# Softmax weights times v: from a high/low float32r pair to plain float32, with one PSUM bank per head and a new order of work

## The chip, the cores and the metric

One core of one Trainium2 chip runs the whole layer in one launch. The metric is device time in microseconds (us), the median of repeated executions of the same program. All arithmetic is float32 or close to it: the kernel keeps the precision of float32 products on TensorE by splitting operands into a high and a low part.

## The reference

One layer of a hybrid encoder over 512 positions of 1,024 channels. The parts in full detail below are those that the change touches.

```python
def reference(x, mem, ...):
    h = rms_norm(x, norm_mix_pre)
    z = h @ w_in                                  # 1024 x 6144
    u_s, q, k, v, g = split(z)                    # 1024 each, g 2048
    ys = s5_branch(u_s, ...)                      # 64 groups x 64 complex states, scan over positions
    ys = gelu(ys); ys = ys * sigmoid(ys @ w_glu + b_glu)
    ya = diff_attention(q, k, v, ...)
    merged = g_a * (ys @ w_ssm_proj) + g_b * (ya @ w_da_proj)
    x = x + rms_norm(merged @ w_mix_out, ...)
    x = x + rms_norm(memory_cross_attention(...), ...)      # 4 heads, 256 memory tokens
    x = x + rms_norm(square(relu(rms_norm(x) @ w_ff1)) @ w_ff2, ...)

# diff_attention, 8 heads, two softmaxes of 64 channels each, 128 channels of v, blocks of 128 queries:
    p = softmax(where(k_chunk <= q_chunk, q k^T / 8, -inf))
    w = p[:, :, 0] - lam * p[:, :, 1]
    o = w @ v
    o = o * rsqrt(mean(o * o, axis=-1) + EPS) * head_norm * (1 - lam_init)
```

## The kernel before, in words

Every big product is made of float32r products. An operand X is kept as a high part (X cast to float32r) and a low part (X minus the high part), and a product of two such operands is three products on TensorE (`trip`): high by low, low by high, high by high. Weights stream in from HBM in pieces of 128x1024 (`wload`); ScalarE makes the high part `whi`, VectorE or GpSimd the low part `wlo` (`wsplit`).

The order of work is set while the program is recorded. Each part of the work is a Python generator with a rank; `step` always advances the generator of lowest rank whose next instruction could start, by a table of costs and latencies, no later than a little after the time at which TensorE has come (`SLACK`). The big projections are the filler (`filler`, rank 1000): they go to TensorE whenever nothing of lower rank is ready. The ranks are the constants `R_...`; `BX` and `BW` are biases that decide, phase by phase, whether VectorE or GpSimd takes an operation that both could do; `ULEAD` and `GL` say how many of the u and gate projections stand ahead of and behind each head's q and k projection. Each engine then works through its own list in order, and waits where an operand isn't there. All DMAs are issued by one queue, SyncE's, in order.

The first 400 us or so hold, side by side:

- the projections for v, u, q, k and the gates (48 pieces of weights, 24 products each);
- the S5 branch in eight groups m (`ssm_pre`, `ssm_mid`, `ssm_main`). In `ssm_main` TensorE first multiplies the group's u with a small table (the rows `ps<-u,ga`, 16 float32 products), VectorE scans the states, and TensorE then makes the outputs (`ps<-st,C` and `ps<-u,Dt`, 16 products each). u comes back from HBM in another layout into `u2`, and the table `Dt` comes from HBM too; there is one buffer for each, so a group's loads wait until the group before has made its outputs;
- the differential attention, head by head. `rope` rotates q and k in one pair of buffers (`ropeB`, `ropeA`) and copies the result by DMA into `q02`, `k02` and so on, of which there is one set (`QB = 1`): a head's copies wait until the head before has made its last scores, and k's rotation waits until q's copies have read the buffer. `attn_block` makes the scores of a block of 128 queries, both softmax numerators, their difference `w`, transposes it on TensorE, and multiplies it with v. `attn_head` then sums, normalizes and transposes the head's output.

In weights times v (`attn_block`, from L1031) the transposed weights are split into `wth` (ScalarE) and `wtl` (VectorE), and v was kept as high and low part side by side in the tile `vy` (`evac_v`, `evac_rows`). For each block of 128 keys TensorE makes two products into one PSUM region of 256 columns: `wth` with both parts of v (256 columns), and `wtl` with the high part of v (128 columns). A head has two PSUM banks; `attn_head` copies the second halves out, adds the first halves to them (tile `on`), squares, and brings in the softmax sum `sm0` as a factor: its reciprocal is applied twice to the sum of squares and once to the result. The rsqrt is a power of -1/2 on GpSimd (`rstd`).

After the S5 branch come the gated unit (`glu`; its input is split from `mt` into `g2h` and `g2l` by `gelu`), the merge, the output projection, the cross-attention and the MLP; from about 400 us on the kernel is nearly all large products.

Of the kernel before, what the change touches and what calls it, by code (L numbers as in the profile page):

```python
# [31 lines left out]
HEADS = 8  # L32
# [40 lines left out]
WTB = 2  # L73
# [26 lines left out]
class Kern:  # L100
# [889 lines left out]
    def attn_block(self, pool, h, i, po, sm0, qk, vv, todo, fin):  # L990
        q2, k2 = qk
        km, rows = P * (i + 1), slice(P * i, P * i + P)
        v = self.V
        sm = yield from self.small(4)
        sm1 = yield from self.small(2)
        p = yield from self.alloc(pool, [P, 2, SEQ], "p", bufs=PBUF)
# [26 lines left out]
        w = p[:, 0, :km]  # L1023
# [11 lines left out]
        while len(po) <= i // 2:  # L1035
            po.append((yield from self.bank("o")))
        yield (None, self.rdy(wh, wl, vv))
        o = po[i // 2][:, 2 * P * (i % 2):2 * P * (i % 2) + 2 * P]
# [4 lines left out]
        self.drop(wh, wl)  # L1043
        fin.append(i)

    def attn_head(self, pool, h, Q, yo, vv, ya):
        v = self.V
# [4 lines left out]
        sm0, ss4, rs = sm[:, 0:4], sm[:, 4:8], sm[:, 8:12]  # L1052
        fin, po, todo = [], [], [8]
# [3 lines left out]
        ya[h] = yo  # L1057
        on = yield from self.alloc(pool, [P, 4, P], "on")
# [12 lines left out]
        yield from self.rstd(ss4, 4, 1.0 / P, EPS, rs)  # L1071
        yield from v.tensor_tensor(out=rs, in0=rs, in1=sm0, op=ALU.mult)
        for i in range(4):
            yield from self.A.activation(out=on[:, i], in_=on[:, i], func=AF.Copy, scale=rs[:, i:i + 1])
        self.drop(sm)
# [195 lines left out]
    def build(self):  # L1271
# [8 lines left out]
        vp = self.open("vy")  # L1280
# [396 lines left out]
```

## Time and profile before

| | us |
|---|---|
| median of 3 runs (1103.91 to 1105.7) | 1104.45 |
| the profiled execution's own time | 1103.1 |
| its span, first to last instruction | 1101.2 |
| TensorE busy | 1062.3 (96% of the span) |
| VectorE busy | 696.8 (63%) |
| ScalarE busy | 510.7 (46%) |
| GpSimd busy | 100.7 (9%) |
| mean granted TensorE clock, of full speed | 0.993 |

The profile is one execution, so a sum over its rows is made against 1103.1 us; the median lies 1.35 us above it. A large product of 128x512 takes about 390 ns from start to end, but they overlap: a new one starts every 223 to 227 ns. Engine names in the rows: PE is TensorE (PEld its weight loads), DVE VectorE, ACT ScalarE, POOL GpSimd, SPq the DMA queue of SyncE.

### The profile page before, as it was taken

To read this page: it belongs to the slowest core of one execution; us is meant where nothing else is said; L and a number is where in the kernel's file an instruction comes from. 1 tells how busy PE (TensorE), PEld (TensorE's weight loads), DVE (VectorE), ACT (ScalarE), POOL (GpSimd) and SP (SyncE) were. 2 spreads that over 40 slices of the span, in tenths; PEclk is the share of its full clock that TensorE was granted. 3 is DMA by queue.
4 is the path that set the end of the run, shared out by engine and by line. 5 is a ranking of instruction groups with operands and counts; after the bars stand their busy time and mean duration, and the time that the engine had idled before them with its cause. 6 is when DMAs were issued, how large, how long until landed. Compare 5 with 4: busy or idle time off the path is not lost.

```text
span 1101.2 us, 15716 instructions
## 1 busy us (share of the span) xinstructions
PE 1062.3 (96%) x5854; PEld 884.5 (80%) x5854; DVE 696.8 (63%) x1242; ACT 510.7 (46%) x989; POOL 100.7 (9%) x104
## 2 busy tenths in 40 slices
PE   8999899999979889999999999999999999999997
PEld 7888777787768668888889888889888888888885
DVE  5899999999998777444469555466443223444234
ACT  5556465666556776322256444354432213443121
POOL 5300121012200030000014000011000000000001
PEclk9999999999989999999999999999999999999999
DMA  7556556664545674444555521314333233333222
GB/s 266 163 161 186 153 142 171 168 164 138 158 124 144 169 174 123 144 143 143 191 173 173 173 95 58 99 57 133 98 97 102 99 101 97 96 96 96 96 76 77
DMA packets 96044, 146.38 MB, mean 133 GB/s; under 512 B 45665, under 2 KB 57441, under 8 KB 95969
## 3 DMA queue, kind: packets, MB, share of 16 engines
q1 hardware_dynamic: 95968, 145.39, 44.8%
q8 instruction: 46, 0.75, 0.3%
q14 instruction: 30, 0.24, 0.1%
HBM read 120.87 MB, written 11.91 MB: 121 GB/s over the span
## 4 chain that ended last, share of the span: by engine, by line
PE 71%; DVE 16%; DMA 4%; issue 3%; ACT 3%; SPq 2%; POOL 1%; POOLq 0%; DVEq 0%; ACTq 0%
PE ps L364 70%; DVE rr L95 2%; SPq L215 2%; DVE wlo L95 2%; DVE ga L95 2%; DVE sm L95 2%; DVE ropeA L95 1%; PE ps L373 1%; DMA scr_g<-gt 1%; DMA mt<-scr_y 1%; DVE st L95 1%; DMA Dt<-sk 1%; ACT ropeB L95 1%; DVE ev L95 1%; ACT whi L95 1%
## 5 line engine op out<-in xcount | busy, mean ns | idle before, releaser
L95 DVE TENSOR_TENSOR wlo<-wraw,whi 128x1024 fp32r<-128x1024 f32 x171 | 210.0, 1228 | 278.8 <-ACT whi L95 278.5
L95 ACT CAST whi<-wraw 128x1024 fp32r<-128x1024 f32 (+1 forms) x180 | 185.9, 1033 | 296.0 <-PE ps L364 269.8
L364 PE MATMUL ps<-hTl,whi 128*128 128x512 f32 (+1 forms) x736 | 286.6, 389 | 1.0 <-DVE sm L95 1.0
L364 PE MATMUL ps<-hTh,whi 128*128 128x512 f32 (+1 forms) x736 | 280.9, 382 | 0.0
L364 PE MATMUL ps<-hTh,wlo 128*128 128x512 f32 (+1 forms) x736 | 280.7, 381 | 0.0
L364 PEld LDWEIGHTS ps<-hTh,whi 128*128 128x128 f32 x736 | 138.7, 189 | 27.3
L364 PEld LDWEIGHTS ps<-hTl,whi 128*128 128x128 f32 x736 | 139.0, 189 | 25.8 <-DVE sm L95 1.2
L364 PEld LDWEIGHTS ps<-hTh,wlo 128*128 128x128 f32 x736 | 139.2, 189 | 23.7
L364 PE MATMUL ps<-whi,vy 128*128 128x512 f32 x384 | 123.5, 389 | 0.0
L364 PE MATMUL ps<-whi,g2l 128*128 128x512 f32 x256 | 99.7, 389 | 0.0
L364 PE MATMUL ps<-wlo,vy 128*128 128x512 f32 x224 | 87.9, 392 | 0.0
L364 PEld LDWEIGHTS ps<-whi,vy 128*128 128x128 f32 x384 | 72.1, 188 | 15.1
L364 PE MATMUL ps<-wlo,g2h 128*128 128x512 f32 x192 | 74.9, 390 | 0.0
L364 PE MATMUL ps<-whi,g2h 128*128 128x512 f32 x192 | 74.7, 389 | 0.0
L364 PE MATMUL ps<-vy,whi 128*128 128x512 f32 (+1 forms) x256 | 65.6, 338 | 0.0
L364 PEld LDWEIGHTS ps<-whi,g2l 128*128 128x128 f32 x256 | 48.1, 188 | 9.7
L95 POOL TENSOR_TENSOR sm<-sm,mhalf 128x1 f32<-128x1 f32 (+1 forms) x28 | 25.9, 925 | 326.9 <-DVE sm L95 292.3
L364 PEld LDWEIGHTS ps<-wlo,vy 128*128 128x128 f32 x224 | 42.1, 188 | 8.4
L364 PEld LDWEIGHTS ps<-vy,whi 128*128 128x128 f32 x256 | 44.5, 189 | 5.0
L95 ACT COPY ropeB<-ps 32x512 f32<-32x512 f32 x64 | 37.0, 578 | 14.1 <-DMA q<-ropeB 11.2
L364 PE MATMUL ps<-vy,wlo 128*128 128x512 f32 (+1 forms) x128 | 43.0, 336 | 0.0
L364 PEld LDWEIGHTS ps<-whi,g2h 128*128 128x128 f32 x192 | 36.0, 188 | 7.6
(235 smaller groups left out, 1618.3 us busy)
## 6 DMA issues: line engine op xcount, KB each, us to landing
wraw<-in_wall_dram SPq DMA_DIRECT2D x172, 512.0 KB, 3.5
xr<-in_x_dram SPq DMA_DIRECT2D x8, 512.0 KB, 4.9
q<-ropeB SPq DMA_DIRECT2D x32, 128.0 KB, 3.1
scr_g<-gt SPq DMA_DIRECT2D x16, 256.0 KB, 3.5
Dt<-sk SPq DMA_DIRECT2D x64, 64.0 KB, 3.3
gl<-scr_g SPq DMA_DIRECT2D x16, 256.0 KB, 3.8
gain<-in_gains_dram SPq DMA_DIRECT2D x5, 512.0 KB, 5.3
xt<-in_xT_dram SPq DMA_DIRECT2D x8, 256.0 KB, 5.2
```

The costliest lines, as they stand in the source:

```text
L95: getattr(k.eng[best], "copy" if (best, m) == ("ACT", "tensor_copy") else m)(**kw)
L215: self.nc.sync.dma_start(out=out, in_=in_)
L364: self.nc.tensor.matmul(out, lhsT=lhsT, rhs=rhs, start=start, stop=stop, **kw)
L373: self.nc.tensor.transpose(out, in_, self.ident)
```

## The change

- v is kept once, as float32: `evac_v` scales the PSUM bank by four activations of 128 columns, one per head, and there is no low part. Each head has a tile of its own.
- The transposed weights are copied once by ScalarE into a float32 tile `wt`; `wtl` is gone. For each block of keys TensorE makes one float32 product of 128 columns. A head has one PSUM bank.
- `attn_head` reads that bank directly: no sum of two halves. Squares are taken with a scale of 1/sqrt(128). With s the softmax sum, the result is o * (mean(o^2) + EPS * s^2)^(-1/2), which is the same as dividing o by s first; two small VectorE operations take the place of five.
- The ranks, `SLACK`, `BW` and `ULEAD` have new values, so that the recorded order of the first 400 us differs on every engine.

```diff
-SLACK = 1800.0
+SLACK = 1400.0
-R_TAB, R_PRE, R_ROT, R_MID, R_MAIN, R_U, R_ATT, R_BLK, R_ROPE, R_GATE, R_W = 1, -0.3, -0.55, -0.3, -0.5, 0, 0, 0, 0, 0, -0.55
+R_TAB, R_PRE, R_ROT, R_MID, R_MAIN, R_U, R_ATT, R_BLK, R_ROPE, R_GATE, R_W = 1, 0.1, -0.55, -0.6, -0.5, -0.5, -0.45, 0, 0, -0.3, -0.55
-BW = (1000,400,1000,200,100,400,600,400)
+BW = (200,200,700,200,100,400,600,400)
-ULEAD = (1,2,2,2,1,0,0,0)
+ULEAD = (2,2,2,2,0,0,0,0)
...
-            o = [vv[:, 4 * nh:4 * nh + 4, b, i] for i in range(2)]
-            yield from self.evac_rows(ps.rearrange("p (h e) -> p h e", h=4), o[0], o[1], self.rs[:, b:b + 1])
+            for h in range(4):
+                yield from self.A.activation(out=vv[4 * nh + h][:, b], in_=ps[:, h * P:h * P + P], func=AF.Copy,
+                                             scale=self.rs[:, b:b + 1])
+            self.unbank(ps)
...
-        wh = yield from self.alloc(pool, [P, SEQ], "wth", F32R, bufs=WTB)
-        wl = yield from self.alloc(pool, [P, SEQ], "wtl", F32R, bufs=WTB)
-        yield from self.split(wh[:, :km], wl[:, :km], pt[:, :km])
+        wt = yield from self.alloc(pool, [P, SEQ], "wt", bufs=WTB)
+        yield from self.A.copy(out=wt[:, :km], in_=pt[:, :km])
...
         for kb in range(i + 1):
             c = slice(kb * P, kb * P + P)
-            self.mm(o, wh[:, c], vv[:, kb].rearrange("p x e -> p (x e)"), kb == 0, False)
-            self.mm(o[:, :P], wl[:, c], vv[:, kb, 0], False, kb == i)
+            self.mm(po["b"][:, rows], wt[:, c], vv[:, kb], kb == 0, kb == i)
...
-        for j in range(2):
-            o4 = po[j].rearrange("p (i x e) -> p i x e", i=2, x=2)
-            yield from self.A.copy(out=on[:, 2 * j:2 * j + 2], in_=o4[:, :, 1])
-            yield from v.tensor_tensor(out=on[:, 2 * j:2 * j + 2], in0=o4[:, :, 0], in1=on[:, 2 * j:2 * j + 2], op=ALU.add)
-        self.unbank(*po)
+        o4 = po["b"].rearrange("p (i e) -> p i e", i=4)
...
-            yield from self.A.activation(out=sq, in_=on[:, i], func=AF.Square, accum_out=ss4[:, i:i + 1])
+            yield from self.A.activation(out=sq, in_=o4[:, i], func=AF.Square, scale=P ** -0.5, accum_out=ss4[:, i:i + 1])
...
-        yield from v.reciprocal(out=sm0, in_=sm0)
-        yield from v.tensor_tensor(out=ss4, in0=ss4, in1=sm0, op=ALU.mult)
-        yield from v.tensor_tensor(out=ss4, in0=ss4, in1=sm0, op=ALU.mult)
-        yield from self.rstd(ss4, 4, 1.0 / P, EPS, rs)
-        yield from v.tensor_tensor(out=rs, in0=rs, in1=sm0, op=ALU.mult)
+        yield from v.scalar_tensor_tensor(out=sm0, in0=sm0, scalar=EPS, in1=sm0, op0=ALU.mult, op1=ALU.mult)
+        yield from v.tensor_tensor(out=ss4, in0=ss4, in1=sm0, op=ALU.add)
+        yield from self.G.tensor_tensor(out=rs, in0=ss4, in1=self.mhalf, op=ALU.pow)
```

Three places of the recorded order, before and now.

The start, on VectorE: `hTl` is the low part of a slice of x, `wlo` that of half a piece of weights. Before, GpSimd made the first eight halves of `wlo`, and VectorE began with:

```order
L95 SCALAR_TENSOR_TENSOR hTl_82<-xt_157,vecs_89,hTh_81 128x512
L95 SCALAR_TENSOR_TENSOR hTl_82<-xt_160,vecs_89,hTh_81 128x512
L95 SCALAR_TENSOR_TENSOR hTl_82<-xt_164,vecs_89,hTh_81 128x512
L95 SCALAR_TENSOR_TENSOR hTl_82<-xt_167,vecs_89,hTh_81 128x512
L95 COPY ga_80<-ga_80 128x32
L95 TENSOR_TENSOR ga_80<-ga_80 128x128
```

Now VectorE makes both:

```order
L95 SCALAR_TENSOR_TENSOR hTl_82<-xt_164,vecs_96,hTh_81 128x512
L95 TENSOR_TENSOR wlo_178<-wraw_163,whi_177 128x512
L95 SCALAR_TENSOR_TENSOR hTl_82<-xt_167,vecs_96,hTh_81 128x512
L95 TENSOR_TENSOR wlo_178<-wraw_163,whi_177 128x512
L95 SCALAR_TENSOR_TENSOR hTl_82<-xt_171,vecs_96,hTh_81 128x512
L95 TENSOR_TENSOR wlo_227<-wraw_170,whi_226 128x512
```

The eight halves of `wlo` moved from GpSimd to VectorE, each behind a low part of x.

The seventh of the S5 groups, on TensorE: from the last output products of the sixth group (`u,Dt`) to the first product of the seventh (`u,ga`, which needs the new `u2`). Before:

```order
L364 MATMUL ps_3560<-st_146,C_2785 64x64 x2
L364 MATMUL ps_3560<-u_525_3230,Dt_3221 64x64 x2
L364 MATMUL ps_3541<-vy_83,wth_3553 128x256
L364 MATMUL ps_3541<-vy_83,wtl_3554 128x128
L364 MATMUL ps_3626<-u_590_3624,ga_80 64x64 x16
```

Now there are 20 rows between them; the last of these, up to the `u,ga`, are:

```order
L364 MATMUL ps_3585<-k_519_3193,q_500_3048 128x512
L364 MATMUL ps_3585<-kh_107_645,ql_105_643 128x512
L373 MATMUL ps_3584<-ident_91,p_3484 128x128 x3
L364 MATMUL ps_3489<-vy_8_87,wt_3578 128x128 x2
L364 MATMUL ps_3489<-vy_8_87,wt_3592 128x128 x3
L364 MATMUL ps_3628<-hTl_82,whi_3310 128x512
L364 MATMUL ps_3628<-hTh_81,wlo_3311 128x512
L364 MATMUL ps_3628<-hTh_81,whi_3310 128x512
L364 MATMUL ps_3551<-u_578_3549,ga_80 64x64 x16
```

Before, four weights-times-v products stood between the two; now there are 12 projection products, four score products, five transposes and five weights-times-v products.

The seventh head's q and k, on SyncE's queue. Before:

```order
L215 DMA q_671_4114<-ropeB_3956 64x512 x2
L215 DMA ql_96_601<-ropeA_3993 64x512
L215 DMA q_672_4115<-ropeB_3956 64x512 x2
L215 DMA ql_97_602<-ropeA_3993 64x512
L215 DMA wraw_4139<-in_wall_dram 128x1024
L215 DMA scr_g_124<-gt_4122 128x512
L215 DMA wraw_4211<-in_wall_dram 128x1024
L215 DMA k_694_4277<-ropeB_4134 64x512
```

Now:

```order
L215 DMA q_660_4025<-ropeB_3787 64x512 x2
L215 DMA ql_104_642<-ropeA_3881 64x512
L215 DMA q_661_4026<-ropeB_3787 64x512 x2
L215 DMA ql_105_643<-ropeA_3881 64x512
L215 DMA wraw_4060<-in_wall_dram 128x1024
L215 DMA k_677_4153<-ropeB_4033 64x512
```

One piece of weights is loaded between q's copies and k's where two and a gate's store were. On TensorE, between the sixth head's last scores and the seventh head's first, there are 33 projection products where there were 66.

## Rows read from the trace of the kernel before

**Rows 1.** The page: busy time by engine, and VectorE in 40 slices.
```profile
PE 1062.3 (96%) x5854; PEld 884.5 (80%) x5854; DVE 696.8 (63%) x1242; ACT 510.7 (46%) x989; POOL 100.7 (9%) x104
...
DVE  5899999999998777444469555466443223444234
```

**Rows 2.** Windows: length, then busy PE, PEld, DVE, ACT, POOL; granted clock, DMA, GB/s.
```profile
300.00:325.00 25.00, 17.61 (x180) 14.86 (x178) 22.34 (x46) 14.13 (x32) 1.20 (x1) 0.86 0.48 127
...
450.00:475.00 25.00, 25.00 (x112) 20.68 (x111) 11.49 (x14) 6.52 (x7) 0.00 (x0) 1.00 0.41 145
```

**Rows 3.** TensorE's waits: line, released by what: us in total, times, longest.
```profile
PE ps L364 <- DMA u<-scr_u: 7.9, 3, 7.4
PE ps L373 <- DVE p L95: 3.6, 4, 1.7
...
PE ps L364 <- DVE g2l L95: 2.6, 2, 2.0
PE ps L364 <- DVE wtl L95: 1.7, 3, 0.8
PE ps L373 <- DVE sm L95: 1.6, 1, 1.6
```

**Rows 4.** Timeline of TensorE, weights times v: start us, duration us, operation.
```profile
430.84 0.34 PE L364 MATMUL ps<-vy,wth 128*128 128x256 f32 x1
...
431.07 0.34 PE L364 MATMUL ps<-vy,wth 128*128 128x256 f32 x1
```

**Rows 5.** Timeline of TensorE, float32 products of the S5 branch.
```profile
288.86 0.67 PE L364 MATMUL ps<-C,bb 128*32 128x128 f32 x16
...
308.83 0.29 PE L364 MATMUL ps<-u,Dt 128*64 128x64 f32 x4
...
310.46 0.29 PE L364 MATMUL ps<-u,Dt 128*64 128x64 f32 x4
```

**Rows 6.** The tiles wth and wtl: operation and count, duration ns min/median/max, first and last start.
```profile
L364 PEld LDWEIGHTS ps<-vy,wth x80: 186/188/190, 103.2 to 432.6; 128*128 128x128 f32 x80
...
L95 DVE TENSOR_TENSOR wtl<-ps,wth x32: 276/498/690, 102.3 to 430.2; 128x128 fp32r<-128x128 f32 x8, 128x256 fp32r<-128x256 f32 x8, 128x384 fp32r<-128x384 f32 x8, 128x512 fp32r<-128x512 f32 x8
```

**Rows 7.** Groups by line and shape: busy us, mean ns of one, idle before.
```profile
L95 DVE TENSOR_TENSOR on<-ps,on 128x256 f32<-128x256 f32 x16 | 6.4, 416 | 1.7 <-ACT on L95 1.7
L95 DVE SCALAR_TENSOR_TENSOR vy<-ps,rs,vy 128x512 fp32r<-128x512 f32 x8 | 5.9, 743 | 1.0 <-ACT vy L95 1.0
L95 DVE TENSOR_TENSOR sm<-sm 128x4 f32<-128x4 f32 x24 | 4.7, 196 | 4.2 <-POOL sm L95 3.9
...
L95 ACT ACTIVATE on<-on,sm 128x128 f32<-128x128 f32 x32 | 10.3, 395 | 9.4 <-DVE sm L95 9.4
```

**Rows 8.** Timeline of the start.
```profile
5.82 1.27 POOL L95 TENSOR_TENSOR wlo<-wraw,whi 128x512 fp32r<-128x512 f32 x1 [3.21 <-ACT whi L95]
...
7.15 0.50 PE L364 MATMUL ps<-wlo,hTh 128*128 128x512 f32 x1 [1.52 <-POOL wlo L95]
```

**Rows 9.** Timelines of TensorE (two batches of u,ga) and of SyncE's queue.
```profile
285.32 1.15 PE L364 MATMUL ps<-u,ga 128*64 128x64 f32 x32
...
318.74 1.98 PE L364 MATMUL ps<-u,ga 128*64 128x64 f32 x32 [7.38 <-DMA u<-scr_u]
...
310.79 4.44 SPq L215 DMA_DIRECT2D Dt<-sk  x8
315.28 0.43 SPq L215 DMA_DIRECT2D u<-scr_u  x1
```

**Rows 10.** Timeline of TensorE at the hand-overs to the fifth and seventh head.
```profile
291.44 0.30 PE L364 MATMUL ps<-k,q 128*128 128x128 f32 x1 [1.33 <-DMA k<-ropeA]
...
350.50 0.39 PE L364 MATMUL ps<-kh,ql 128*128 128x512 f32 x1
...
371.65 0.30 PE L364 MATMUL ps<-k,q 128*128 128x128 f32 x1 [0.62 <-DMA k<-ropeA]
```

**Rows 11.** Timeline of VectorE, the gated unit's low parts.
```profile
391.76 2.72 DVE L95 TENSOR_TENSOR g2l<-mt,g2h 128x512 fp32r<-128x512 f32 x1
...
396.25 1.09 DVE L95 TENSOR_TENSOR g2l<-mt,g2h 128x512 fp32r<-128x512 f32 x1 [0.16 <-ACT g2h L95]
```

More of the change, by code (lines that the diff above doesn't have):

```diff
@@ L1030, in attn_block, with attn_head @@
         self.drop(p)
-        wh = yield from self.alloc(pool, [P, SEQ], "wth", F32R, bufs=WTB)
-        wl = yield from self.alloc(pool, [P, SEQ], "wtl", F32R, bufs=WTB)
-        yield from self.split(wh[:, :km], wl[:, :km], pt[:, :km])
+        wt = yield from self.alloc(pool, [P, SEQ], "wt", bufs=WTB)
+        yield from self.A.copy(out=wt[:, :km], in_=pt[:, :km])
         self.unbank(pt)
[L1035 to L1038, printed above, removed]
+        while "b" not in po:
+            if not po:
+                po["w"] = True
+                po["b"] = yield from self.bank("o")
+            else:
+                yield lambda: "b" in po
+        yield (None, self.rdy(wt, vv))
         for kb in range(i + 1):
             c = slice(kb * P, kb * P + P)
-            self.mm(o, wh[:, c], vv[:, kb].rearrange("p x e -> p (x e)"), kb == 0, False)
-            self.mm(o[:, :P], wl[:, c], vv[:, kb, 0], False, kb == i)
-        self.drop(wh, wl)
+            self.mm(po["b"][:, rows], wt[:, c], vv[:, kb], kb == 0, kb == i)
+        self.drop(wt)
         fin.append(i)
-    def attn_head(self, pool, h, Q, yo, vv, ya):
+    def attn_head(self, pool, h, Q, vp, vv, ya):
         v = self.V
@@ L1052, in attn_head @@
         sm0, ss4, rs = sm[:, 0:4], sm[:, 4:8], sm[:, 8:12]
-        fin, po, todo = [], [], [8]
+        fin, po, todo = [], {}, [8]
         for i in range(4):
@@ L1056, in attn_head @@
         yield lambda: len(fin) == 4
-        ya[h] = yo
-        on = yield from self.alloc(pool, [P, 4, P], "on")
-        for j in range(2):
-            o4 = po[j].rearrange("p (i x e) -> p i x e", i=2, x=2)
-            yield from self.A.copy(out=on[:, 2 * j:2 * j + 2], in_=o4[:, :, 1])
-            yield from v.tensor_tensor(out=on[:, 2 * j:2 * j + 2], in0=o4[:, :, 0], in1=on[:, 2 * j:2 * j + 2], op=ALU.add)
-        self.unbank(*po)
+        ya[h] = self.t(vp, [P, 2, SEQ], f"vy{h}", F32R)
+        o4 = po["b"].rearrange("p (i e) -> p i e", i=4)
         sq = yield from self.alloc(pool, [P, P], "sq")
         for i in range(4):
-            yield from self.A.activation(out=sq, in_=on[:, i], func=AF.Square, accum_out=ss4[:, i:i + 1])
+            yield from self.A.activation(out=sq, in_=o4[:, i], func=AF.Square, scale=P ** -0.5, accum_out=ss4[:, i:i + 1])
         self.drop(sq)
-        yield from v.reciprocal(out=sm0, in_=sm0)
-        yield from v.tensor_tensor(out=ss4, in0=ss4, in1=sm0, op=ALU.mult)
-        yield from v.tensor_tensor(out=ss4, in0=ss4, in1=sm0, op=ALU.mult)
-        yield from self.rstd(ss4, 4, 1.0 / P, EPS, rs)
-        yield from v.tensor_tensor(out=rs, in0=rs, in1=sm0, op=ALU.mult)
+        yield from v.scalar_tensor_tensor(out=sm0, in0=sm0, scalar=EPS, in1=sm0, op0=ALU.mult, op1=ALU.mult)
+        yield from v.tensor_tensor(out=ss4, in0=ss4, in1=sm0, op=ALU.add)
+        yield from self.G.tensor_tensor(out=rs, in0=ss4, in1=self.mhalf, op=ALU.pow)
+        on = yield from self.alloc(pool, [P, 4, P], "on")
         for i in range(4):
-            yield from self.A.activation(out=on[:, i], in_=on[:, i], func=AF.Copy, scale=rs[:, i:i + 1])
+            yield from self.A.activation(out=on[:, i], in_=o4[:, i], func=AF.Copy, scale=rs[:, i:i + 1])
+        self.unbank(po["b"])
         self.drop(sm)
@@ L1287, in build @@
         rh, rl = (lambda k: hT[0][:, k]), (lambda k: hT[1][:, k])
-        vall = self.t(vp, [P, HEADS, 2 * SEQ], "vy", F32R)
-        vv = vall.rearrange("p h (k x e) -> p h k x e", k=4, x=2)
+        vv = [self.t(vp, [P, 2 * SEQ], f"vy{h}")[:, :SEQ].rearrange("p (k e) -> p k e", k=4) for h in range(HEADS)]
         self.quotas(mm=6, t=2, s=0, o=0)
@@ L1358, in build @@
         for h in range(HEADS):
-            self.spawn(self.attn_head(ap, h, Q, vall[:, h].rearrange("p (x t) -> p x t", x=2), vv[:, h], ya), R_ATT)
+            self.spawn(self.attn_head(ap, h, Q, vp, vv[h], ya), R_ATT)
         self.run(lambda: "tables" in S)
@@ L1424, in build @@
         dp = self.open("mix")
-        vt = vall.rearrange("p h (i t) -> p h i t", i=4)
-        mT, kT = ([vt[:, m, i:i + 2] for m in range(8)] for i in (0, 2))
+        mT, kT = ([ya[m][:, i].rearrange("p (j t) -> p j t", j=2) for m in range(8)] for i in range(2))
         g_post, g_pre = (self.gain(dp, i) for i in (1, 2))
@@ L1507, in ff1_fill @@
             fb = [self.t(g2p, [P, KB, SEQ], "g2" + x, F32R) for x in "hl"]
-            fa = vall.rearrange("p h (x t) -> p h x t", x=2)
-            f = [[fa[:, m, i] if m < 8 else fb[i][:, m - 8] for m in range(16)] for i in range(2)]
+            f = [[ya[m][:, i] if m < 8 else fb[i][:, m - 8] for m in range(16)] for i in range(2)]
             F = set()
```

## The prediction

> **What bounds the kernel.** I read the busy shares first. TensorE is busy 1062.3 of 1101.2 us and idle for 38.9 [rows 1]; everything else can only matter through those 38.9 us, or through products that come or go. VectorE's row of slices is full in the first third and far from it afterwards [rows 1], so the next view is windows: from about 400 us on a window of 25 us holds 25.00 us of TensorE work (112 products starting every 0.223 us), while at 300 to 325 us there are 17.61, with VectorE busy for 22.34 and the granted clock at 0.86 [rows 2]. So the place is the first 400 us, where the S5 branch, the attention and the projections share the engines, and which is also what the change rewrites. Third, the waits of TensorE [rows 3]: 7.9 us for u coming back from HBM, 7.4 of it one wait; 3.6 and 1.6 us for VectorE ahead of the transposes of the softmax weights; 1.7 us for the low half of the transposed weights; 2.6 us for the gated unit's low parts. No single engine is the bound: TensorE does the work, and VectorE and SyncE's queue decide where it stops.
>
> **The change, part by part.** The measure is the profiled execution, 1103.1 us.
>
> (1) *Weights times v on TensorE.* 80 blocks of keys, each before a product of 256 and one of 128 columns, [rows 6] for the count. A pair takes 0.23 us, from 430.84 to 431.07 [rows 4]. No row shows a float32 product of the full array with 128 columns. The nearest are the S5 branch's: from 308.83 to 310.46 there are 14 rows of 4 records; a float32 product leaves two records (the 16 of u,ga stand as x32), so 28 products took 1.63 us, two side by side, or 0.116 us for 64 columns in one place, 0.233 for 128 [rows 5]. The product `C,bb` has 128 columns: eight, four side by side, in 0.67 us, at most 0.335 each with filling and draining [rows 5]. I take 0.24, near the first, which is a steady flow: 80 x 0.01 = **+0.8 us**. Low end: columns cost nothing beyond the 0.116, -9.1 us. High end: two weight loads of 0.188 [rows 6] one after the other, 0.376, +11.7 us.
>
> The Trainium skill (page "FP8 and Floating Point Precision", section "TensorE Precision Notes") says that true FP32 takes four passes through the array. At 2.4 GHz that is an estimate of 4 x 128 columns = 0.213 us against 384 columns = 0.160 us for the pair, so by it the change would cost 4.3 us. The trace differs on the pair: short products don't go at the rate of their columns there, it takes 0.23 and not 0.160 [rows 4]; with the page's 0.213 alone the term would be -1.4 instead of +0.8.
>
> (2) *The start.* The first product waits 1.52 us for a `wlo` that GpSimd takes 1.27 us over [rows 8]. VectorE, by its 0.416 us for 256 columns [rows 7], needs about 0.7, but makes a low part of x first: **-0.5 us**, between +0.5 and -0.9.
>
> (3) *The low half of the weights.* `wtl` is gone, and with it the 1.7 us that TensorE waited for it [rows 3]: **-1.7 us**; 0 if the next wait stands right behind. The copy `wt` on ScalarE is the old `wth`.
>
> (4) *u for the S5 groups.* The wait of 7.38 us at 318.74 is a hand-over: the sixth group's outputs free the buffers at 310.7, the queue then issues eight loads of `Dt` (4.44 us), then u, which lands at 318.7 [rows 9]: 8.2 us. In the order before, only four short products stood there. Now it is 12 projections x 0.223, four score products of about the same, five weights-times-v at 0.24 and five transposes of 0.1: 5.3 us, a wait of 2.9. The eighth group's cover becomes 24 x 0.223 and some 1.7 us of short products, 7.1: a wait of 1.1. Of the other five, two have covers of 8.0 and 8.2 (0.2 together), the rest more. 4.2 against 7.9 us: -3.7. Behind the long wait the clock was at its lower level, 1.2 GHz (0.86 on average in that window, [rows 2]): the batch of u,ga took 1.98 us where another took 1.15 [rows 9]. -0.8, taking it that a wait of 2.9 us does not end in a lower clock; 0 if it does. Together **-4.5 us**; 0 if the 8.2 us become 12.
>
> (5) *The hand-over from head to head.* One set of q and k buffers: after the last scores, q's copies go out, free the rotation's buffers, k is rotated, its copies go out, then the next scores start. To the seventh head this took from 350.9 to 371.65, 20.8 us, and ended in a wait of 0.62; to the fifth in one of 1.33 [rows 10], each with a second one behind it: the cover was just too short. The new order cuts the cover: to the seventh head 33 fewer projections (7.4 us) and two fewer weights-times-v (0.5), to the fifth 18 fewer (4.0), six fewer (1.4) and four transposes (0.4): 7.9 and 5.8 us. What speaks against paying all of it: k's rotation is VectorE work that stood in VectorE's list, and in SyncE's queue one load stands between q's copies and k's where there were three transfers. I take **+1.0 us**; from -2 (both waits gone) to +13.7 (all the cover lost is waited for).
>
> (6) *VectorE's list.* Removed: 32 `wtl` x 0.49 = 15.8 [rows 6], 16 sums x 0.416 = 6.7, eight passes over v x 0.743 = 5.9, 16 of 24 operations of 128x4 x 0.196 = 3.1 [rows 7]: 31.5 us. Added, by the order's counts, from GpSimd: some 8,000 columns beyond the start's, at 0.416 us per 256, 13.1 us. That leaves 18 of some 300 busy us. The waits for VectorE ahead of the transposes are 3.6 + 1.6 = 5.2 us [rows 3]; half of it, **-2.6 us**, between 0 and all of it: a list that is 6% shorter doesn't end every wait, but those were short.
>
> (7) *The gated unit's first products* waited 2.6 us for `g2l` [rows 3]. Two of the eight low parts were GpSimd's; while it made them, VectorE's own took 2.72 us where one alone took 1.09 [rows 11]. All eight are VectorE's now: **-1.0 us**, from 0 to -2.6.
>
> At nothing: ScalarE's eight passes over v become 32 of 128 columns at about 0.395 [rows 7], some 7 us more, and 16 copies fall away for about as much; ScalarE is busy for 14.13 of 25 us in the window with the most idle time of TensorE [rows 2]. If that cover were gone, the v banks would come free later while the projections hold others. The head's PSUM bank is held longer, through the normalization, but a head needs one of two now.
>
> Sum: +0.8 - 0.5 - 1.7 - 4.5 + 1.0 - 2.6 - 1.0 = -8.5 us: 1094.6 on the profiled execution. The median of the runs lies 1.35 us higher, so **1096.0 us**.
>
> **Rivals.** *A, the hand-over between heads becomes the longest wait.* Place: the first scores of the seventh and the fifth head. Price: if the hand-overs take what they took, the waits grow by the cover lost, 13.7 us, and a lower clock behind them costs the 0.8 that (4) gives back: -8.5 - 1.0 + 14.5 = +5.0, **1109.5 us**. For it: both waits were already bare [rows 10]. Against it: 20.8 us is more than the links need, and VectorE's list is shorter. It decides where the hand-over to the seventh head takes over some 17 us.
>
> *B, the float32 product is dearer.* At the 0.335 us of `C,bb` [rows 5] it costs 8.4 instead of 0.8: -0.9, **1103.6 us**. For it: that row has the same 128 columns; against: eight products with a drain at either end.
>
> *C, the waits only move.* A new order opens waits that the old one happened to cover; if (3), (6) and (7) give nothing and (4) half, the sum is -0.5 + 0.8 - 2.3 + 1.0 = -1.0, **1103.5 us**. It is also the case in which the change does its work off the critical path. Against it: the 7.4 us are one wait with a clear cause.
>
> **How the numbers follow.** A run of this kernel can be told from no change at about 0.2%, 2.2 us. My own case 0.73, A 0.13, B 0.05, C 0.09. The own case's range is 1087 to 1102: down by the low ends of (1), (4), (6), up by those of (3) and (6). The range for 8 in 10 goes from 1087 over B and C to 1108, and leaves out A and a little below. Faster 0.73 (the own case); within 0.2% 0.14 (B and C); slower 0.13 (A).
>
> **What would show it.** Right: the first u,ga of the seventh group waits 2 to 4 us and not 7; the products `vy,wt` start 0.23 to 0.25 us apart; no wait for VectorE between transposed weights and the product with v; VectorE some 15 us less busy; from 450 us on nothing differs. Wrong: over 5 us of waits for k or kh at one head's first scores (A); 0.3 us or more between the starts of `vy,wt` (B); TensorE's idle time as long as before with other releasers (C).

## The result, and the profile after

The changed kernel takes 1088.49 us (median of four runs, 1087.76 to 1090.12), the kernel before 1105.08 us in runs on the same chip (1103.91 to 1105.75). The ratio is 0.9853, with a 95% interval from 0.9836 to 0.987: 16.6 us faster, where the forecast was 8.5. The profiled execution of the changed kernel is the slowest of its four, 1090.12 us with a span of 1088.4; against the profiled execution of before this is 13.0 us, and rows can account for that much.

The page of the changed kernel: busy time by engine.

```profile
PE 1060.7 (97%) x5854; PEld 884.0 (81%) x5854; DVE 675.5 (62%) x1184; ACT 508.7 (47%) x997; POOL 67.5 (6%) x82
```

Against [rows 1] TensorE's work is the same to 1.6 us, its idle time falls from 38.9 to 1088.4 - 1060.7 = 27.7 us, and VectorE is busy for 21.3 us less. Windows tell where. The columns are those of [rows 2]; first the kernel before, then the changed one, each cut about where its S5 branch and attention end.

```profile
0.00:400.00 400.00, 370.66 (x2510) 301.94 (x2510) 355.56 (x741) 245.12 (x549) 68.34 (x71) 0.99 0.61 165
400.00:1101.00 701.00, 691.69 (x3347) 582.58 (x3345) 341.28 (x502) 265.62 (x441) 32.41 (x34) 1.00 0.36 114
```

```profile
0.00:387.00 387.00, 368.61 (x2509) 301.10 (x2510) 339.48 (x699) 245.52 (x566) 36.51 (x49) 0.99 0.63 170
387.00:1088.00 701.00, 692.08 (x3347) 582.89 (x3345) 336.00 (x487) 263.13 (x432) 30.97 (x33) 1.00 0.36 115
```

The same 2,510 records of products (2,509 in the changed trace) are done by 387 us instead of 400; the 701 us behind are equal. So the whole gain lies in the first part, and there it is mostly waiting that went: TensorE's idle time fell from 29.3 to 18.4 us and its busy time by 2.1. The waits of TensorE in the changed kernel:

```profile
PE ps L364 <- DVE g2l L95: 4.2, 3, 2.1
PE ps L364 <- ACT wt L95: 3.3, 4, 1.2
PE ps L373 <- DVE p L95: 1.6, 3, 0.7
PE ps L373 <- DVE sm L95: 1.6, 2, 0.9
...
PE ps L364 <- DMA u<-scr_u: 1.3, 2, 0.9
...
PE ps L364 <- DMA kh<-ropeB: 0.8, 3, 0.3
```

Against [rows 3], the 7.9 us for u are 1.3; no single wait is over 2.1 us; and the largest entry is now the gated unit's low parts. The window of [rows 2] at 300 us looks like this now, with TensorE at 21.70 instead of 17.61 and the clock at its upper level (1.00 for 0.86); the second row is the deepest hole that is left, at the gated unit:

```profile
300.00:325.00 25.00, 21.70 (x177) 16.69 (x173) 23.93 (x47) 16.79 (x43) 1.92 (x3) 1.00 0.58 161
...
371.00:380.00 9.00, 5.53 (x23) 3.85 (x22) 8.96 (x15) 7.87 (x15) 0.00 (x0) 0.86 0.91 212
```

The timeline of TensorE in the changed kernel, at the places that the prediction named and, last, at a group of products of weights with v that no wait precedes (start, duration, operation, and in brackets the idle time before it and its releaser):

```profile
6.86 0.50 PE L364 MATMUL ps<-wlo,hTh 128*128 128x512 f32 x1 [0.71 <-DVE wlo L95]
...
300.69 0.29 PE L364 MATMUL ps<-u,Dt 128*64 128x64 f32 x4
...
304.18 0.52 PE L373 MATMUL ps<-ident,p 128*128 128x128 f32 x3 [0.47 <-ACT bb L95]
305.57 0.71 PE L364 MATMUL ps<-vy,wt 128*128 128x128 f32 x4 [0.88 <-ACT wt L95]
306.88 0.94 PE L364 MATMUL ps<-vy,wt 128*128 128x128 f32 x6 [0.60 <-ACT wt L95]
307.57 0.48 PE L364 MATMUL ps<-hTl,whi 128*128 128x512 f32 x1
...
309.15 1.15 PE L364 MATMUL ps<-u,ga 128*64 128x64 f32 x32
...
342.62 0.39 PE L364 MATMUL ps<-kh,ql 128*128 128x512 f32 x1
...
357.89 0.22 PE L364 MATMUL ps<-k,q 128*128 128x128 f32 x1
358.33 0.33 PE L364 MATMUL ps<-kh,ql 128*128 128x128 f32 x1 [0.21 <-DMA kh<-ropeB]
...
375.38 0.50 PE L364 MATMUL ps<-g2l,whi 128*128 128x512 f32 x1 [1.39 <-DVE g2l L95]
...
378.43 0.80 PE L364 MATMUL ps<-g2l,whi 128*128 128x512 f32 x1 [2.08 <-DVE g2l L95]
...
411.99 1.05 PE L364 MATMUL ps<-vy,wt 128*128 128x128 f32 x8
412.80 0.48 PE L364 MATMUL ps<-g2l,whi 128*128 128x512 f32 x1
```

These rows are read step by step after the experiments.

### The profile page after: what moved, and what is told of

Read it like the earlier page. It is cut to its first block, busy times and chain, and to the rows that moved or that the text cites. A ratio compares the mean times of both kernels' runs of the same rounds, so it can differ in the third digit from the quotient of the medians.

```text
span 1088.4 us, 15608 instructions
## 1 busy us (share of the span) xinstructions
PE 1060.7 (97%) x5854; PEld 884.0 (81%) x5854; DVE 675.5 (62%) x1184; ACT 508.7 (47%) x997; POOL 67.5 (6%) x82
## 4 chain that ended last, share of the span: by engine, by line
PE 78%; DVE 10%; DMA 4%; ACT 3%; issue 2%; SPq 2%; DVEq 0%; POOLq 0%; ACTq 0%
PE ps L364 77%; PE ps L373 2%; DVE wlo L95 2%; SPq L215 2%; DVE ga L95 1%; DVE rr L95 1%; DVE sm L95 1%; DMA Dt<-sk 1%; ACT ropeB L95 1%; DMA kh<-ropeB 1%; ACT whi L95 1%; DVE ropeA L95 1%; DMA q<-ropeB 0%; DMA wraw<-in_wall_dram 0%; DVE gt L95 0%
## 5 line engine op out<-in xcount | busy, mean ns | idle before, releaser
L95 DVE TENSOR_TENSOR wlo<-wraw,whi 128x1024 fp32r<-128x1024 f32 (+1 forms) x180 | 216.8, 1204 | 291.5 <-ACT whi L95 291.2
L95 POOL TENSOR_TENSOR sm<-sm,mhalf 128x1 f32<-128x1 f32 (+1 forms) x28 | 27.6, 988 | 359.9 <-DVE sm L95 359.9
L95 ACT ACTIVATE p<-ps,sm 128x128 f32<-128x128 f32 (+2 forms) x64 | 33.6, 528 | 22.9 <-DVE sm L95 22.3
L364 PEld LDWEIGHTS ps<-wlo,g2h 128*128 128x128 f32 x192 | 36.0, 188 | 7.6
```

The costliest lines, as they stand in the source:

```text
L95: getattr(k.eng[best], "copy" if (best, m) == ("ACT", "tensor_copy") else m)(**kw)
L364: self.nc.tensor.matmul(out, lhsT=lhsT, rhs=rhs, start=start, stop=stop, **kw)
```

## The experiments

Two accounts stood against each other. By the first, the gain is the sum of the change's parts: less VectorE work, a better cover for u. By the second, it belongs to the recorded order as a whole: each order opens and closes waits all over the first 400 us, and the change has a good one. Each kernel was timed beside the kernel before, on the same chip. One table serves all the readings. The columns from the span on belong to one execution of each kernel, the profiled one; the clock is its mean granted clock. The last two columns are worked out: loss = idle time + span x (1 - clock), and work = span - loss.

| kernel | median us | ratio to before, 95% | span | PE busy | idle | clock | loss | work |
|---|---|---|---|---|---|---|---|---|
| before | 1103.78 to 1105.08 | 1 | 1101.2 | 1062.3 | 38.9 | 0.993 | 46.6 | 1054.6 |
| changed | 1088.49 | 0.9853 (0.9836 to 0.987) | 1088.4 | 1060.7 | 27.7 | 0.995 | 33.1 | 1055.3 |
| new arithmetic, old constants | 1105.34 | 1.0003 (0.9991 to 1.0016) | 1104.8 | 1065.8 | 39.0 | 0.989 | 51.2 | 1053.6 |
| old arithmetic, new constants | 1117.93 | 1.0115 (1.0095 to 1.0136) | 1115.8 | 1074.7 | 41.1 | 0.984 | 59.0 | 1056.8 |
| one float32r product | 1089.77 | 0.9859 (0.984 to 0.9878) | 1087.6 | 1054.6 | 33.0 | 0.992 | 41.7 | 1045.9 |
| VectorE pass added | 1099.69 | 0.9955 (0.9939 to 0.997) | 1099.9 | 1065.5 | 34.4 | 0.990 | 45.4 | 1054.5 |
| changed, old `ULEAD` | 1104.94 | 1.0008 (0.9993 to 1.0023) | 1104.9 | 1066.5 | 38.4 | 0.987 | 52.8 | 1052.1 |
| changed, old ranks | 1117.83 | 1.0123 (1.0103 to 1.0143) | 1116.3 | 1070.8 | 45.5 | 0.982 | 65.6 | 1050.7 |
| changed, old `BW` | 1088.94 | 0.9872 (0.9853 to 0.989) | 1086.8 | 1059.2 | 27.6 | 0.996 | 31.9 | 1054.9 |
| changed, `SLACK` 1500 | 1104.45 | 1.0004 (0.9991 to 1.0017) | 1103.1 | 1066.7 | 36.4 | 0.989 | 48.5 | 1054.6 |
| changed, `SLACK` 1350 | 1099.86 | 0.995 (0.993 to 0.9971) | 1098.7 | 1065.5 | 33.2 | 0.990 | 44.2 | 1054.5 |
| before without `wtl` | 1098.22 | 0.9934 (0.9913 to 0.9955) | 1095.1 | 1057.1 | 38.0 | 0.990 | 49.0 | 1046.1 |
| before, `SLACK` 1700 | 1106.63 | 1.0016 (1.0001 to 1.0032) | 1105.2 | 1070.3 | 34.9 | 0.989 | 47.1 | 1058.1 |
| before, new `ULEAD` | 1108.52 | 1.003 (1.0018 to 1.0042) | 1105.2 | 1066.6 | 38.6 | 0.987 | 53.0 | 1052.2 |

Work lies between 1050.7 and 1058.1 us in every kernel that makes all products, and in the two that leave some out it is some 9 us less. What tells the orders apart is the loss, from 31.9 to 65.6 us. A wait counts twice in it: TensorE stands still, and the rows behind the longer ones show it at the lower level of its clock. The loss is an estimate. A step of 0.001 in the clock is 1.1 us, and the clock differs between executions of one kernel: in 55 executions of the kernel before, timed beside these kernels, it lies between 0.983 and 0.993, at 0.988 in the middle, and the row in the table has 0.993. At 0.988 its loss would be some 52 us instead of 46.6. The changed kernel's four executions lie between 0.995 and 0.997. So the loss parts the changed kernel from the kernel before, but a difference of a few us between two rows decides nothing.

**The new arithmetic alone.** The changed kernel with the four old constants.

```diff
-SLACK = 1400.0
+SLACK = 1800.0
-R_TAB, R_PRE, R_ROT, R_MID, R_MAIN, R_U, R_ATT, R_BLK, R_ROPE, R_GATE, R_W = 1, 0.1, -0.55, -0.6, -0.5, -0.5, -0.45, 0, 0, -0.3, -0.55
+R_TAB, R_PRE, R_ROT, R_MID, R_MAIN, R_U, R_ATT, R_BLK, R_ROPE, R_GATE, R_W = 1, -0.3, -0.55, -0.3, -0.5, 0, 0, 0, 0, 0, -0.55
-BW = (200,200,700,200,100,400,600,400)
+BW = (1000,400,1000,200,100,400,600,400)
-ULEAD = (2,2,2,2,0,0,0,0)
+ULEAD = (1,2,2,2,1,0,0,0)
```

> The new arithmetic with the old ranks, SLACK, BW and ULEAD. The trace of the changed kernel shows TensorE's waits for u down from 7.9 to 1.3 us, for k and kh from 4.0 to 0.8, for p and sm from 5.2 to 3.2, and for the transposed weights up from 1.7 to 3.3. Theory 'both': shorter VectorE work gives a third of the 16 us, the order the rest: 1098 to 1101 us. Rival 'order alone': the arithmetic is worth nothing off the critical path: 1103 to 1107 us. Rival 'arithmetic alone': 1088 to 1091 us.

Measured: 1105.34 us, no change, as the rival "order alone" had it. VectorE is busy for 677.8 us, about as in the changed kernel, the wait for u has gone as well, and nothing is won. TensorE's waits in this kernel, and the longest on its timeline:

```profile
PE ps L373 <- DVE p L95: 9.1, 6, 5.0
PE ps L364 <- ACT wt L95: 5.9, 4, 2.8
...
PE ps L364 <- DMA u<-scr_u: 1.8, 2, 1.5
```

```profile
216.26 1.75 PE L373 MATMUL ps<-ident,p 128*128 128x128 f32 x7 [5.04 <-DVE p L95]
```

The 6 us that u gave back stand ahead of the transposes (`p`, 9.1 us for 3.6) and of the products of weights with v, one of them as a wait of 5.04 us that the kernel before did not have.

**The new constants alone.** The kernel before with the four new constants (the same lines, the other way).

```diff
-SLACK = 1800.0
+SLACK = 1400.0
...
-ULEAD = (1,2,2,2,1,0,0,0)
+ULEAD = (2,2,2,2,0,0,0,0)
```

> The old arithmetic (pair of float32r products, wtl, two banks per head) with the new ranks, SLACK, BW and ULEAD. 'Both': 1093 to 1097 us. 'Order alone': 1087 to 1091 us. 'Arithmetic alone': 1103 to 1107 us. If the two parts need each other (the ranks fit only the shorter VectorE list), it is no faster than before, and e1 isn't either.

Measured: 1117.93 us, 1.15% slower, outside every range that was named; only the sentence on two parts that need each other fits. Its longest wait in total:

```profile
PE ps L364 <- DVE wtl L95: 5.4, 6, 2.6
```

Here the wait for `wtl` is 5.4 us instead of 1.7 [rows 3]. The parts do not add: 0 and +13 us alone, -16.6 together.

**The price of the float32 product.** The order of the changed kernel is held, and each product of weights with v becomes a single float32r product of high parts; the low parts of the weights and of v are left out of the result.

```diff
-        wt = yield from self.alloc(pool, [P, SEQ], "wt", bufs=WTB)
+        wt = yield from self.alloc(pool, [P, SEQ], "wt", F32R, bufs=WTB)
...
-            self.mm(po["b"][:, rows], wt[:, c], vv[:, kb], kb == 0, kb == i)
+            self.nc.tensor.matmul(po["b"][:, rows], lhsT=wt[:, c], rhs=vv[:, kb], start=kb == 0, stop=kb == i)
+            self.note("PE", 214.0, [po["b"][:, rows]], [wt[:, c], vv[:, kb]])
...
```

> The changed kernel in its own recorded order, with weights times v as a single float32r product of the high parts; the low parts of the weights and of v are left out. It prices the float32 product against a product that reads the same columns once. The float32 product takes 0.23 us in the trace of the changed kernel; a float32r product of 128 columns starts some 0.06 to 0.17 us after the one before. If TensorE is the limit where these 80 products stand: 80 x 0.06 to 0.17 = 5 to 13 us faster, 1075 to 1083 us. If they stand in stretches where TensorE waits anyway, 0 to 3 us faster.

Measured: 1089.77 us, the changed kernel's time. The timeline shows that TensorE does save: four products from 411.38 to 411.77, 0.10 us each, where four float32 products of the changed kernel go from 411.99 to 412.80, 0.20 us each.

```profile
411.38 0.56 PE L1045 MATMUL ps<-vy,wt 128*128 128x128 f32 x4
411.77 0.44 PE L364 MATMUL ps<-g2l,whi 128*128 128x512 f32 x1
```

```profile
PE ps L1045 <- ACT wt L95: 5.5, 5, 2.3
PE ps L364 <- DVE g2l L95: 5.2, 3, 2.1
PE ps L373 <- DVE p L95: 2.7, 4, 1.1
```

By these rows 80 x 0.105 = 8.4 us leave TensorE's work (9.4 in the table), and the loss grows by 8.6 (idle time 33.0 for 27.7 us, clock 0.992 for 0.995): the waits for `wt`, `g2l` and `p` take up what the products set free. In this order the float32 product is not what sets the end of the first part.

**VectorE's work put back.** The order of the changed kernel is held, and the 32 subtractions return to VectorE, into a tile that nobody reads; the table of costs is not told of them.

```diff
         yield from self.A.copy(out=wt[:, :km], in_=pt[:, :km])
+        wx = self.t(pool, [P, SEQ], "wx", bufs=2)
+        self.nc.vector.tensor_tensor(out=wx[:, :km], in0=pt[:, :km], in1=wt[:, :km], op=ALU.subtract)
```

> The changed kernel with 32 subtractions on VectorE over the transposed weights (the old wtl work, 15.8 us in all) put back into its recorded order; nobody reads their results, but each holds a PSUM bank. Theory 'a full VectorE list costs time': half of it or more comes back, 8 to 16 us slower, 1096 to 1104 us. Rival 'VectorE's list has room now': 0 to 3 us slower.

Measured: 1099.69 us, 11.2 more than the changed kernel. VectorE's busy time rose by 11.8 us (687.3), so that it was paid for nearly in full. The added operation as the view of its tile has it, and TensorE's waits:

```profile
L1036 DVE TENSOR_TENSOR wx<-ps,wt x32: 278/493/692, 114.8 to 423.1; 128x128 f32<-128x128 f32 x8, 128x256 f32<-128x256 f32 x8, 128x384 f32<-128x384 f32 x8, 128x512 f32<-128x512 f32 x8
```

```profile
PE ps L373 <- DVE p L95: 5.4, 5, 1.7
...
PE ps L364 <- DVE st L95: 3.3, 4, 2.2
...
PEld ps L364 <- DVE wx L1036: 1.0, 2, 0.7
```

`p` went from 1.6 to 5.4 and `st` from 1.0 to 3.3 us, with no wait over 2.2. The added pass also keeps its PSUM bank until it is done, as `wtl` did; only 1.0 us of TensorE's weight loads wait for that (the last row), so the price is that of VectorE's time in the main. In the changed order, then, 11.8 us of VectorE's time cost 11.2 us of the kernel's.

**The same relief in the old order.** In the kernel before, the 32 subtractions and their 80 products are left out (the weights' low part is missing from the result); the table of costs still counts them (`dry`: booked, but not issued), so that the order stays.

```diff
...
+            if not dry:
+                getattr(k.eng[best], "copy" if (best, m) == ("ACT", "tensor_copy") else m)(**kw)
...
-        yield from self.split(wh[:, :km], wl[:, :km], pt[:, :km])
+        yield from self.hi(wh[:, :km], pt[:, :km])
+        yield from self.V.tensor_tensor(dry=True, out=wl[:, :km], in0=pt[:, :km], in1=wh[:, :km].bitcast(F32), op=ALU.subtract)
...
-            self.mm(o[:, :P], wl[:, c], vv[:, kb, 0], False, kb == i)
+            self.note("PE", 107.0, [o[:, :P]], [wl[:, c], vv[:, kb, 0]])
```

> The kernel before in its own recorded order, with the 32 subtractions that make wtl and their 80 products left out (the low part of the weights is missing from the result; every other instruction stands where it stood). It is the mirror of the added pass in the changed kernel's order, which cost 11 us. 'A shorter VectorE list saves time in any order': 6 to 12 us faster, 1092 to 1098 us, and u's 7.4 us wait stays. Rival 'only in the changed order, where nothing else waits longer': 0 to 3 us faster, 1101 to 1105 us.

Measured: 1098.22 us against 1104.18, -6.0, at the edge of the range for a shorter list in any order. VectorE is busy for 11.1 us less, as much as the pass above added. But the rows put the gain elsewhere. Without its partner a product of 256 columns takes 0.12 us (four from 322.37 to 322.84) where the pair took 0.23 [rows 4], so that 80 x 0.11 = 8.8 us of TensorE's work are gone, more than the gain. TensorE's idle time hardly fell, 38.0 us against 38.9, and the long wait is there as before:

```profile
312.56 1.97 PE L365 MATMUL ps<-u,ga 128*64 128x64 f32 x32 [6.73 <-DMA u<-scr_u]
...
322.37 0.64 PE L365 MATMUL ps<-vy,wth 128*128 128x256 f32 x4
322.84 0.40 PE L365 MATMUL ps<-hTl,whi 128*128 128x512 f32 x1
```

The experiment removes two things at once, so it does not measure VectorE's share: the products alone could account for all of the gain, and the run with one float32r product showed that such a saving can also vanish in waits. What it does show is that in the old order a shorter list left the waits as long in sum: those for `p` and `wtl` went from 5.3 to 2.8 us, and those for k and `st` from 4.8 to 7.0.

**One constant at a time, from the changed kernel.** First `ULEAD`, then the eleven ranks, then `BW`, each back to its old value.

```diff
-ULEAD = (2,2,2,2,0,0,0,0)
+ULEAD = (1,2,2,2,1,0,0,0)
```

> The changed kernel with the old ULEAD alone (u projections spread to the fifth head). Theory 'the recorded order is a draw': any change of the order of the first 400 us opens some waits and closes others, so each constant undone alone loses some 5 to 15 us, whatever its purpose: 1093 to 1104 us. Rival 'one constant carries the gain': if it is this one (it brings u earlier), 1098 us or more here and 1091 or less in the other three runs of this set.

```diff
-R_TAB, R_PRE, R_ROT, R_MID, R_MAIN, R_U, R_ATT, R_BLK, R_ROPE, R_GATE, R_W = 1, 0.1, -0.55, -0.6, -0.5, -0.5, -0.45, 0, 0, -0.3, -0.55
+R_TAB, R_PRE, R_ROT, R_MID, R_MAIN, R_U, R_ATT, R_BLK, R_ROPE, R_GATE, R_W = 1, -0.3, -0.55, -0.3, -0.5, 0, 0, 0, 0, 0, -0.55
```

> The changed kernel with the old ranks alone (u, attention heads, gates and the S5 tables back at their old ranks; SLACK, BW and ULEAD new). 'A draw': 1093 to 1104 us. 'One constant carries it', these ranks: 1098 us or more, the other three of the set at 1091 or less.

```diff
-BW = (200,200,700,200,100,400,600,400)
+BW = (1000,400,1000,200,100,400,600,400)
```

> The changed kernel with the old BW alone: GpSimd again makes low parts of weights in the first stretches, the start among them. By itself this is 0.3 us at the start (first large product at 6.86 instead of 7.15 us) and some 10 us of VectorE work; it leaves TensorE's order nearly as it is. 'A full VectorE list costs time' (the added pass of 15.8 us cost 11): moving work back to GpSimd relieves VectorE, so 1085 to 1090 us, no slower than the changed kernel. 'A draw': 1093 to 1104 us. 'One constant carries it': 1098 us or more.

Measured: 1104.94, 1117.83 and 1088.94 us. With the old `ULEAD` the whole gain is gone, with the old ranks it is worse than before by 1.2%, and `BW` is worth nothing that shows: it moves some work back to GpSimd (79.3 us busy instead of 67.5) and leaves VectorE's busy time (674.8) and TensorE's list nearly as they were. None of the three lies in the range of a draw, 1093 to 1104, and no single constant carries the gain. The old value of `SLACK`, 1800, was not run by itself. With the old ranks the wait for u is back:

```profile
PE ps L364 <- DMA u<-scr_u: 6.6, 3, 5.7
```

**`SLACK` a little to either side.** Still the changed kernel.

```diff
-SLACK = 1400.0
+SLACK = 1500.0
```

> The changed kernel with SLACK 1500 instead of 1400, a value of neither kernel: how much the time scatters for a small change that has no purpose. 'A draw': anything from 1088 to 1104 us, away from the changed kernel by over 3 us. 'One constant carries it', or an order that is good for reasons that a small step keeps: 1086 to 1091 us.

```diff
-SLACK = 1400.0
+SLACK = 1350.0
```

> The changed kernel with SLACK 1350, the other side of 1400 from the run at 1500. 'A draw': 1095 to 1118 us, as three of four neighbours. It could also beat both kernels (below 1087 us), which a draw allows in perhaps 1 of 10 cases.

Measured: 1104.45 and 1099.86 us. A step of 100 in one number takes all of the gain, a step of 50 the other way two thirds of it. Nothing in these runs shows a value of `SLACK` that one could reason to; a step deals the order anew. With 1500 the waits are others again:

```profile
PE ps L364 <- ACT wt L95: 6.6, 3, 3.4
...
PE ps L373 <- ACT on L95: 4.6, 1, 4.6
```

**Other orders for the old arithmetic.** The kernel before with `SLACK` at 1700, and with the new `ULEAD`, which by the first account shortens the wait for u.

```diff
-SLACK = 1800.0
+SLACK = 1700.0
```

> The kernel before with SLACK 1700 instead of 1800, a small step without a purpose. 'Both kernels are picks among orders that scatter by 10 us and more': 1110 to 1122 us, as the old arithmetic gave 1118 with the new ranks. Rival 'the old arithmetic isn't sensitive': 1102 to 1108 us.

```diff
-ULEAD = (1,2,2,2,1,0,0,0)
+ULEAD = (2,2,2,2,0,0,0,0)
```

> The kernel before with the new ULEAD alone. 'Both are picks': 1110 to 1122 us. Rival 'bringing u earlier is what removes the 7.4 us wait': 1096 to 1100 us.

Measured: 1106.63 and 1108.52 us. Neither is the 1110 or more that two picks from a wide scatter would have given, nor is the second the 1100 or less of a wait for u that is gone: these two steps move the old arithmetic by 2 and 4 us, where steps of `SLACK` moved the changed kernel by 11 and 16. With the new `ULEAD` the wait for u still takes 6.5 us, now in four pieces, and `p` 6.9 instead of 3.6:

```profile
PE ps L364 <- DMA u<-scr_u: 6.5, 4, 3.1
```

What follows from all of them: both accounts hold in part. Seven kernels with the new arithmetic (the first two of nearly the same order) gave 1088.5, 1088.9, 1099.9, 1104.5, 1104.9, 1105.3 and 1117.8 us, and four of the old one 1104 to 1105, 1106.6, 1108.5 and 1117.9. The best of the one lies 16 us under the best of the other, but the middle ones of either kind lie at 1104.5 and at 1106.6 to 1108.5, not far apart. Both are needed for the 1088 us: VectorE's removed work put back costs 11.2 us in this order, and undoing `ULEAD` or the ranks, or moving `SLACK`, takes most or all of the gain. That no order of the old arithmetic reaches it is not shown, with four tried. No kernel that computes everything was clearly faster than the changed one; that with the old `BW` is equal to it within the intervals. Open: which of the eleven ranks matters, why this order opens so few waits, whether a longer search would find an equally good order for the old arithmetic, and how the 6 us of the kernel without `wtl` divide between TensorE and VectorE.

## Why the prediction was right, and where it was not

The sign, the range (1087 to 1108, with the result 1.5 us inside its lower end) and the place were right: nothing differs behind 400 us. The forecast was half as large as the gain. On the two profiled executions it was 8.5 against 13.0; the other 3.6 of the 16.6 us are only where these two executions stand among their runs. Part of the sign is luck. The steps price the old order's waits, place by place, as the new order changes them; that the new order opens few others was taken, not worked out, and of the seven kernels with the new arithmetic three gained nothing and one lost 1.2%. By the steps of the prediction:

(1) *The float32 product*: three products from 306.88 to 307.57 (six records) took 0.23 us each, and four from 411.99 to 412.80, behind no wait, 0.20; a pair before took 0.23 [rows 4]. About 0 instead of +0.8; work differs by 0.7 us in the table. Rival B is out. The Trainium skill (page "FP8 and Floating Point Precision", section "TensorE Precision Notes") has four passes for true FP32, which gave the estimate of 0.213 us; the trace agrees, with 0.20 to 0.23. The cost of 4.3 us that followed from it did not come, since the pair, at 0.23 us, does not go at the rate of its columns.

(2) *The start*: the first product went from 7.15 [rows 8] to 6.86 us, -0.3 for -0.5. Right.

(3) *The low half of the weights*: 1.7 us were to go. `wtl` went, and TensorE waits 3.3 us for `wt` from ScalarE instead. Of these, 1.5 (at 305.57 and 306.88) lie within the hand-over of u and are counted there; that leaves +0.1. The step's own upper end, 0 because the next wait stands right behind, was the case: the products now follow the copy of the weights too closely. "No wait for VectorE between transposed weights and product" was true, and did not help.

(4) *u*: the chain of loads took again 8.2 us, as worked out: the sixth group's outputs free the buffers at 300.9, u is issued at 306.05 and lands 3.0 later. SyncE's queue there, in the changed kernel:

```profile
301.02 4.99 SPq L215 DMA_DIRECT2D Dt<-sk  x8
306.05 0.43 SPq L215 DMA_DIRECT2D u<-scr_u  x1
```

The cover was to be 5.3 us and the wait 2.9. It was 8.25 us, and `u,ga` at 309.15 waits for nothing, because the waits of 0.47, 0.88 and 0.60 us stand inside the cover. So of 7.38 us idle 1.95 are left there, and they have other names. All waits for u went from 7.9 to 1.3, and those stand at 238.68 and 275.11, not at the seventh and eighth group. The clock came as forecast: `u,ga` took 1.15 us instead of 1.98 [rows 9], the window is at 1.00. But it did not come by the reason given, that a wait of 2.9 us leaves the clock up: no such wait came. At the gated unit, see (7), a wait of 2.08 us close behind one of 1.39 did end in the lower level, while one of 2.02 us there in the kernel before (at 390.36) did not. The term of -4.5 was, with the 1.95 us counted here, 1.95 - 6.6 - 0.8 = -5.4.

(5) *The hand-over from head to head*: forecast +1.0; the waits for k and kh went from 3.4 and 0.6 to 0.8 in all, -3.2. To the seventh head it took from 343.0 to 357.9, 14.9 us instead of 20.8 [rows 10]: k's rotation was done sooner by more than the cover was cut. The prediction put the point from which rival A decides at 17 us, and the wait at the seventh head is 0.21. What failed is taking the old duration as near to what the links need. ScalarE's last pass over q and SyncE's queue, first before, then changed, show what else was in it:

```profile
353.44 0.63 ACT L95 ACTIVATE ropeB<-ropeA 128x512 fp32r<-128x512 f32 x1 [1.62 <-DVE ropeA L95]
354.10 1.13 SPq L215 DMA_DIRECT2D q<-ropeB  x2
368.47 0.48 SPq L215 DMA_DIRECT2D k<-ropeB  x1
```

```profile
335.33 0.63 ACT L95 ACTIVATE ropeB<-ropeA 128x512 fp32r<-128x512 f32 x1 [0.82 <-DVE sm L95]
341.89 1.16 SPq L215 DMA_DIRECT2D q<-ropeB  x2
354.58 0.47 SPq L215 DMA_DIRECT2D k<-ropeB  x1
```

The prediction let the chain begin with the last scores. In the kernel before it did not: q's own rotation was not done until 354.1, and its copies left 3.6 us behind the start of the last scores (350.50). In the changed kernel q had been ready since 336.0, and its first copies, those of the first softmax, left 0.7 us ahead of that point (342.62). That is 4.3 us; from q's first copies to k's it took 12.7 us instead of 14.4, another 1.7. So k's copies left 6.0 us sooner behind the last scores, while TensorE came to the next scores 5.3 us sooner (it would have been more, but waits of 0.92, 0.62 and 0.74 us for other things stand in between). What in the new order brought q's rotation forward was not tested.

(6) *VectorE's list*: 21.3 us shorter (18 forecast). The waits for `p` and `sm` went from 5.2 to 3.2, -2.0 for -2.6: right on its rows. As a price of VectorE's work it was too narrow: put back, the pass cost 11.2 us, spread over `p`, `st` and shorter waits, with the clock behind them (a mean of 0.990 for 0.995). And in the old order the new arithmetic, with all of the relief, gained nothing. No single value would have been right.

(7) *The gated unit*: from 2.6 and 1.1 (the second for GpSimd's own two low parts) to 4.2 us, +0.5 for -1.0, the wrong sign. VectorE's low parts do take 1.1 us instead of up to 2.72 [rows 11], but there are eight of them, and between them stand a low part of weights and small operations of the last head's attention. VectorE's timeline between the first two of these waits, and the window of the product behind the second:

```profile
374.25 1.07 DVE L95 TENSOR_TENSOR g2l<-mt,g2h 128x512 fp32r<-128x512 f32 x1
...
375.85 1.20 DVE L95 TENSOR_TENSOR wlo<-wraw,whi 128x1024 fp32r<-128x1024 f32 x1
...
377.30 1.08 DVE L95 TENSOR_TENSOR g2l<-mt,g2h 128x512 fp32r<-128x512 f32 x1
```

```profile
378.00:380.00 2.00, 1.57 (x4) 1.19 (x5) 2.00 (x5) 0.87 (x1) 0.00 (x0) 0.50 1.08 227
```

VectorE never stops (8.96 of 9 us in the window at 371), and behind the wait of 2.08 us TensorE's product takes 0.80 us at the lower level of the clock (0.50, 1.2 GHz), where the one behind the wait of 1.39 us took 0.50.

The steps as measured are 0 - 0.3 + 0.1 - 5.4 - 3.2 - 2.0 + 0.5 = -10.3 us. What is left of the 13.0 is the clock outside of (4), by its mean some 1.5 us less lost, and small waits that no step named. So (1), (2) and (6) were right within 1 us, (4) was right in kind and 0.9 too small, (5) and (7) had the wrong sign and (3) came to nothing; (5), with 4.2 us, is the step that failed: its error is about the difference between 8.5 and 13.0. The errors of (3) and (7), +1.8 and +1.5 us, happen to be made up by those of (1) and (4) and the 2.7 us that no step named. Rival C, waits that only move, did not come here; it is what the new arithmetic with the old constants does, to the letter: the wait for u goes, and the time stays.

## What to carry to other kernels

Where an order is written down once and engines follow it without looking, price a change of arithmetic and a change of order as one thing: measure the new arithmetic with several orders before believing either, since a single order can hide all of a gain or make one up (here by 16 us). Read the worth of an engine's work in the order in which it will run, by adding the work back with the order held, rather than from the waits that name that engine. And compare orders by TensorE's idle time together with its mean clock: the work itself hardly differs.

## What the runs showed that was not expected

- A change of `SLACK` from 1400 to 1500, in a table of the recording and not in any instruction, costs 16 us, with TensorE's loss going from 33.1 to 48.5 us.
- The busy time of 11 to 12 us on VectorE is worth 11.2 us of the kernel in one order; its removal in another left TensorE's idle time where it was (38.9 and 38.0 us).
- A float32 product of 128x128 by 128 columns takes 0.20 to 0.23 us, a single float32r product of the same size 0.10 us in the same place, so that the float32 one costs here about two of them, and about the same as the pair of 256 and 128 columns.
- The hand-over from head to head looked like a chain from the last scores on, and 3.6 of its 20.8 us were q's rotation being late.
